# A two-layer hybrid encoder: TensorE kept in the recorded order, memory handed out by planned end of use, convolution taps and key copies spread out

## The chip, the cores and the metric

The kernel runs on one core of one Trainium2 chip. The metric is the device time of one execution in microseconds; three executions of the kernel before gave 1992.22, 1995.13 and 1999.15 us, with the median 1995.13.

## What is computed

A trunk of two layers over 256 positions of width 2048, all float32, with a final RMS norm. Each layer, cut to what matters (the rotary and norm details are left out):

```python
h = rms_norm(x, norm_g)
proj = h @ w_in                       # 2048 x (13*512 + 256 + 4*2048)
ya = a_bg * depthwise_conv(a_cg * a_x, conv_a_w) * silu(a_z)      # A: conv of 3
yb = gqa_attention(rope(q), rope(k), v) * silu(b_z)               # B: 8 heads on 2
yc = rwkv7_bidir(h, c_r, c_k, c_v, ...) * silu(c_z)               # C: a scan per direction
u = depthwise_conv(d_val * sigmoid(d_gate), dw_w) + dw_b          # D: conv of 31 taps
yd = silu(layer_norm(u)) * silu(d_z)
g = sigmoid(gates + b_gate)                                       # 4 x 2048 columns
merged = sum over the branches of g[k] * (y[k] @ w_branch[k])
x = x + merged @ w_out
```

## The kernel before

Activations lie transposed, channels on the partitions and the 256 positions along the free axis. Weights stream in once: 612 pieces of 128 x 1024 (306 per layer), called weight halves here, since two make a tile of 128 output channels. SyncE loads each (`raw`), ScalarE rounds it to a `hi` part, VectorE takes the rest as `lo` (`fetch`), and TensorE multiplies `hi` with both parts of the activations (512 columns) and `lo` with the first part (256 columns), eight of each per half (`tile_b`, `wide`; accumulators `mg`). A merge of a branch takes two such gate tiles and one piece of branch weights (`tile_branch`, accumulator `mb`, 24 matmuls of 256 columns). This is the main stream, in the order of `STREAM`: low-rank inputs, the scan's inputs, k and v, the inputs of B and A, those of D, merges of A and B, gates of D, merge of D, gates of C, merge of C, output projection.

Beside it run side jobs, Python generators: `rwkv` with `inverses` and `chunks`, `branch_a`, `branch_b`, `conv_d`, `branch_d`, `normalise`. Their matmuls write small accumulators, `sd`. After each main matmul `pump` lets those side jobs record a step whose time has come. That time is a plan: `Engine` counts a duration for every operation recorded, keeps a clock for VectorE and ScalarE (`clk`), and sets `due`, the time at which a step's results should be there; a job that yields 0 goes on `SLACK` after it, one that yields a number goes on so much later. Inside `rush` an operation counts as started `BUSY` after the present and is recorded with high priority. `drain` lets planned time pass until a job is done.

The recorded order isn't yet the order of the engines. The framework that builds the program simulates it once and orders each engine's instructions by that simulation and by priority; a main matmul may so be placed ahead of a side matmul recorded before it. `manual_schedule(engines=...)` leaves the named engines in the recorded order; before, only `first_x` does that, and not for TensorE.

The scan is done in chunks of 64 positions, two head pairs at a time. In `rwkv`, per chunk, a matmul makes the next state, ScalarE copies it into a block-diagonal tile (`bdS`), TensorE transposes that (`sd<-consts,bdS`), ScalarE copies the result, and so on: a chain that alternates between TensorE and the other two engines, 48 transpositions in the run. `chunks` prepares the operands of the next pair of chunks; it ends with eight copies of transposed keys and values by ScalarE (`bdE<-sd`). `conv_d` does 31 taps on 128 x 256 for each of four channel groups on VectorE (`arena<-arena,par`).

Short-lived tiles come from one large tile, `arena`, that class `Arena` hands out in units of 32 words. `get` looks for a free gap; before, it prefers a gap that holds nothing freed within the last six calls (`RECENT`), then the tightest.

All operations are recorded through one helper, so nearly all rows of the profile name line 204.

Of the kernel before, what the change touches and what calls it, by code (L numbers as in the profile page):

```python
# [102 lines left out]
class Arena:  # L103


    U = 32
    RECENT = 6

    def __init__(self, ap, words):
        self.ap, self.n = ap, words // self.U  # L110
        self.when = np.zeros(self.n, np.int64)
        self.used = np.zeros(self.n, bool)
        self.live = {}
        self.tick = 0
        self.peak = 0

    def get(self, words, keep=False, take=True):

        m = -(-words // self.U)
        self.tick += 1  # L120
        best = None
        i = 0
        while i < self.n:
            if self.used[i]:
                i += 1
                continue
            e = i
            while e < self.n and not self.used[e]:
                e += 1
            if e - i >= m:  # L130

                j = i if keep else e - m
                key = i if keep else (int(self.when[j:e].max()) > self.tick - self.RECENT, e - i - m, -i)
                if best is None or key < best[0]:
                    best = (key, j)
            i = e
        if best is None:
            if not take:
                return False
            raise MemoryError(f"arena: {words} words asked, {(~self.used).sum() * self.U} free, live "  # L140
                              + str(sorted((v[1] * self.U, v[2]) for v in self.live.values())))
        j = best[1]
        if not take:
            return True
        self.used[j:j + m] = True
        self.peak = max(self.peak, int(self.used.sum()) * self.U * 4)
        return j, m
# [1 line left out]
    def free(self):  # L149
        return int((~self.used).sum()) * self.U  # L150

    def put(self, j, m):
        self.tick += 1
        self.used[j:j + m] = False
        self.when[j:j + m] = self.tick


class Side:
# [6 lines left out]
class Engine:  # L165
# [5 lines left out]
    def __getattr__(self, op):  # L171
        f = getattr(self.real, op)

        def call(out, *args, **kw):
            k = self.k
            if op == "preload_act_table_set":
                k.clk["scalar"] = max(k.clk["scalar"], k.now) + 1.3
                return f(out)  # L178
            if op == "dma_start":
                k.landed = max(k.landed, max(k.due, k.now) + k.DMA)  # L180
            elif self.name == "tensor":
                rhs = kw.get("rhs", args[1])
                n = int(np.prod(out.shape[1:]))
                if op == "transpose":
                    k.now += 0.11
                elif rhs.dtype == F32:
                    k.now += max(0.22, n * 4 / 2400 + 0.003)
                else:
                    k.now += max(0.12, n * 0.4445e-3)
                k.due = max(k.due, k.now + 0.2)  # L190
            else:
                n = max(int(np.prod(x.shape[1:])) for x in (out,) + args if hasattr(x, "shape"))
                cost = 0.06 + n / 960 + (0.07 if op == "scalar_tensor_tensor" else 0) if self.name == "vector" else 0.1 + n / 1200 + (0.09 if hasattr(kw.get("scale"), "shape") or hasattr(kw.get("bias"), "shape") else 0)
                cost *= k.INFL
                if self.name in k.clk:
                    start = max(k.clk[self.name], k.now)
                    k.clk[self.name] = start + cost
                    if k.rushing:
                        start = k.next[self.name] = max(k.next[self.name], k.now + k.BUSY)
                        k.next[self.name] += cost  # L200
                    k.due = max(k.due, start) + cost + 0.1
                else:
                    k.due = max(k.due, k.now) + cost
            return f(out, *args, **kw)  # L204

        return call
# [8 lines left out]
class Kern:  # L215
# [1 line left out]
    FAR = 1  # L217
    INFL = 1.05
    RAW = 8
    BUSY = 0.7  # L220
    SLACK = 0.4
    LEAD = 1.7
    TWAIT = 24.0
    XSTEP = 1.0
# [2 lines left out]
    LEAD_A = 2.0  # L227
    LEAD_B = 1.8
    LEAD_D = 1.0
    DMA = 2.5  # L230
    SLABS = 9
    ARENA = (32 + 474 + 32 + 8 - 8 + 16 - 64 + 128 + 16 + 6 - 88 - 16 - 8 - 16 - 32 * FAR - 32 * PARTS - 16) * 32
# [22 lines left out]
    def a(self, shape, keep=False):  # L255
        words = int(np.prod(shape[1:]))
        if self.cur is None:

            t = self.now
            while not self.arena.get(words, keep, False) and self.now < t + 50:  # L260
                self.now += 0.2
                self.pump()
        j, m = self.arena.get(words, keep)
        if self.cur:
            self.cur.purse.net += m * Arena.U
        ap = self.arena.ap[:, j * Arena.U:j * Arena.U + words]
        if len(shape) > 2:
            names = "abcd"[:len(shape) - 1]
            ap = ap.rearrange(f"p ({' '.join(names)}) -> p {' '.join(names)}",
                              **{k: v for k, v in zip(names, shape[1:])})  # L270
        self.arena.live[id(ap)] = (ap, m, str(shape), j)
        return ap
# [9 lines left out]
    def f(self, *aps):  # L282
        for ap in aps:
            _, m, _, j = self.arena.live.pop(id(ap))
            self.arena.put(j, m)
            if self.cur:
                self.cur.purse.net -= m * Arena.U

# [188 lines left out]
    def whole(self, out, ps):  # L477

        nc = self.nc
        nc.scalar.activation(out, ps[:, 1], AF.Copy)  # L480
        nc.vector.tensor_tensor(out, ps[:, 0], out, ALU.add)
        return out


# [244 lines left out]
    def conv_d(self, acc, i, u):  # L729
# [3 lines left out]
        nc.vector.tensor_scalar(a, u[:, 0:S], w(0), self.dwb2[:, i:i + 1], ALU.mult, ALU.add)  # L733
        for j in range(1, 31):
            nc.vector.scalar_tensor_tensor(a, u[:, j:j + S], w(j), a, ALU.mult, ALU.add)
            if j % 3 == 0:
                yield 0.9
        self.f(u)

    def branch_d(self, acc, convs, dz):  # L740
# [357 lines left out]
    def chunks(self, n, out, bd, al, vv, kb, gs, rd):  # L1098
# [30 lines left out]

        nc.tensor.matmul(ps4[:, 2], vv[:, p, ts], self.cen, start=True, stop=True)  # L1130
        nc.tensor.transpose(ps4[:, 3], al[:, p, ts], self.ident)
        for j, src in enumerate((hi, lo)):
            nc.scalar.activation(ex[hi, j, :, CH:], ps4[src, 0:2, CH:], AF.Copy)
            nc.scalar.activation(ex[lo, j, :, CH:], ps4[src, 0:2, 0:CH], AF.Copy)

        for c, src in enumerate((lo, hi)):
            nc.scalar.activation(ex[hi, 2:4, c, CH:], ps4[src, 2:4, CH:], AF.Copy)
            nc.scalar.activation(ex[lo, 2:4, c, 0:CH], ps4[src, 2:4, 0:CH], AF.Copy)
        out.append((ex, mk, w))
        yield 0  # L1140

# [108 lines left out]
    def merge(self, l, br, g, acc, mT, gens):  # L1250
# [10 lines left out]
        psb = self.tile_branch(self.ys[br])  # L1261
        if first:
            acc[g] = self.a([P, 2, S], True)
            nc.vector.scalar_tensor_tensor(acc[g], z, 1.0, psb, ALU.add, ALU.mult)
        else:
            nc.vector.scalar_tensor_tensor(z, z, 1.0, psb, ALU.add, ALU.mult)
            nc.vector.tensor_tensor(acc[g], acc[g], z, ALU.add)
        self.f(z)
        if last:
# [67 lines left out]
    def run(self):  # L1337
# [2 lines left out]
        self.tiles = 0  # L1340
        self.consts()
        self.first_x()
        for l in range(DEPTH):
            self.layer(l)


@with_exitstack
# [122 lines left out]
```

## Time and profile before

| | us |
|---|---|
| median of three executions | 1995.13 |
| the profiled execution | 1995.8 |
| its span, first to last instruction | 1993.9 |
| TensorE matmul busy | 1934.8 |
| TensorE weight load busy | 1716.7 |
| VectorE busy | 1439.8 |
| ScalarE busy | 1268.9 |
| GpSimd busy | 71.6 |

The span is what the rows measure; the execution's own time has 1.9 us around it. Busy time of an engine counts every moment in which one of its instructions is drawn; the end of a matmul is modelled, so two neighbours overlap in the drawing. PE is TensorE, PEld its weight load, DVE VectorE, ACT ScalarE, POOL GpSimd, SP SyncE.

### The profile page before, as it was taken

What the parts mean: (1) busy time and instruction counts of PE and PEld (TensorE: products, weight loads), DVE (VectorE), ACT (ScalarE), POOL (GpSimd) and SP (SyncE); (2) the same over time, 40 slices, a digit from 0 to 9 for tenths busy, and PEclk for the clock granted to TensorE, in tenths of its full rate; (3) what the DMA queues carried; (4) which work ended last, traced back from release to release, by engine and by line L of the source; (5) the groups of instructions that cost most, each with busy time, mean ns of one, the idle gap of its engine ahead of it and who ended that gap; (6) DMA issues with size and microseconds to landing.
All of it is one profiled execution on the core that took longest, in us unless ns stands there. A gap on an engine that the chain in (4) does not pass through costs nothing.

```text
span 1993.9 us, 32440 instructions
## 1 busy us (share of the span) xinstructions
PE 1934.8 (97%) x12194; PEld 1716.7 (86%) x12194; DVE 1439.8 (72%) x2495; ACT 1268.9 (64%) x2293; POOL 71.6 (4%) x117
## 2 busy tenths in 40 slices
PE   8999999899999999999999999998999999999997
PEld 6888788799988898998888887888999989989986
DVE  7867858967787566666677778589787866566655
ACT  6776666567657766554567766766774577565454
POOL 1001010000101000000000010000001100000000
PEclk9999999899999999999999999999999999999998
DMA  7554443344655345566655554533555544456653
GB/s 247 186 181 165 159 156 117 117 165 166 197 181 180 137 150 179 202 206 205 214 186 185 181 169 143 154 114 138 177 171 187 195 143 159 155 184 207 203 190 136
DMA packets 97693, 343.19 MB, mean 172 GB/s; under 512 B 11808, under 2 KB 12192, under 8 KB 97536
## 3 DMA queue, kind: packets, MB, share of 16 engines
q1 hardware_dynamic: 93312, 331.48, 49.1%
q0 software_dynamic: 3648, 8.59, 1.7%
q8 instruction: 96, 1.57, 0.3%
q10 hardware_dynamic: 576, 1.05, 0.1%
q14 instruction: 61, 0.50, 0.1%
HBM read 332.48 MB, written 8.39 MB: 171 GB/s over the span
## 4 chain that ended last, share of the span: by engine, by line
PE 93%; ACT 3%; DVE 2%; DMA 1%; issue 1%; DVEq 0%; SPq 0%; POOL 0%; ACTq 0%; POOLq 0%
PE mg L204 74%; PE sd L204 9%; PE mb L204 9%; DVE arena L204 1%; DVE lo L204 1%; ACT arena L204 1%; ACT bdE L204 1%; DMA raw<-w 1%; ACT hi L204 1%; DMA scratch<-arena 0%; DMA arena<-xT 0%; ACT bdS L204 0%; ACT L178 0%; ACT bdT L204 0%; ACT bdR L204 0%
## 5 line engine op out<-in xcount | busy, mean ns | idle before, releaser
L204 PE MATMUL mg<-slab,hi 128*128 128x512 f32 x4368 | 1113.7, 396 | 17.1 <-DVE slab L204 9.5
L204 DVE TENSOR_TENSOR lo<-raw,hi 128x1024 fp32r<-128x1024 f32 x612 | 746.6, 1221 | 344.1 <-PE mg L204 247.2
L204 PEld LDWEIGHTS mg<-slab,hi 128*128 128x128 f32 x4368 | 789.6, 190 | 160.9 <-DVE slab L204 10.7
L204 ACT ACTIVATE hi<-raw 128x1024 fp32r<-128x1024 f32 x612 | 646.4, 1057 | 440.4 <-PE mg L204 294.7
L204 PE MATMUL mg<-slab,lo 128*128 128x256 f32 x4368 | 618.4, 285 | 1.7 <-DVE lo L204 1.5
L204 PEld LDWEIGHTS mg<-slab,lo 128*128 128x128 f32 x4368 | 585.9, 191 | 37.5 <-DVE lo L204 3.0
L204 DVE TENSOR_TENSOR arena<-arena 128x512 f32<-128x512 f32 (+16 forms) x389 | 166.1, 432 | 35.2 <-ACT arena L204 24.2
L204 DVE SCALAR_TENSOR_TENSOR arena<-arena,par 128x256 f32<-128x256 f32 x346 | 152.2, 479 | 7.8 <-ACT arena L204 6.7
L204 PE MATMUL mb<-slab,hi 128*128 128x256 f32 (+1 forms) x1040 | 156.8, 288 | 1.0 <-DVE slab L204 0.6
L204 PEld LDWEIGHTS mb<-slab,hi 128*128 128x128 f32 x1040 | 141.1, 192 | 5.7 <-DVE slab L204 0.8
L204 DVE TENSOR_TENSOR arena<-mg,arena 128x256 f32<-128x256 f32 x305 | 126.8, 418 | 18.0 <-ACT arena L204 15.3
L204 ACT ACTIVATE arena<-mg 128x256 f32<-128x256 f32 x241 | 89.7, 377 | 67.4 <-PE mg L204 52.3
L204 ACT ACTIVATE arena<-arena 128x256 f32<-128x256 f32 (+4 forms) x195 | 93.5, 497 | 29.5 <-DVE arena L204 26.1
L204 ACT ACTIVATE arena<-arena,b_gate 128x256 f32<-128x256 f32 x128 | 64.0, 503 | 54.9 <-DVE arena L204 54.4
L204 PE MATMUL mb<-slab,lo 128*128 128x256 f32 x528 | 87.2, 286 | 0.0
L178 ACT ACT_TABLE_LOAD x62 | 79.5, 1283 | 8.3 <-PE sd L204 5.0
L204 PEld LDWEIGHTS mb<-slab,lo 128*128 128x128 f32 x528 | 75.1, 192 | 1.6
L204 ACT ACTIVATE bdE<-sd 64x128 f32<-64x128 f32 x256 | 69.7, 272 | 7.5 <-PE sd L204 4.2
L204 DVE SCALAR_TENSOR_TENSOR slab<-arena,slab 128x512 fp32r<-128x512 f32 (+1 forms) x64 | 35.4, 555 | 34.8 <-ACT slab L204 34.7
L204 ACT ACTIVATE arena<-sd 128x64 f32<-128x64 f32 (+4 forms) x122 | 40.0, 332 | 17.3 <-PE sd L204 15.5
L204 DVE SCALAR_TENSOR_TENSOR arena<-arena 128x256 f32<-128x256 f32 (+1 forms) x80 | 37.1, 473 | 17.6 <-ACT arena L204 16.9
L204 PE MATMUL sd<-arena,bdE 128*128 128x128 f32 (+1 forms) x224 | 45.4, 285 | 3.9 <-ACT arena L204 3.3
(96 smaller groups left out, 1062.2 us busy)
## 6 DMA issues: line engine op xcount, KB each, us to landing
raw<-w SPq DMA_DIRECT2D x612, 512.0 KB, 3.3
arena<-xT SPq DMA_DIRECT2D x4, 512.0 KB, 8.3
scratch<-slab POOLq DMA_DIRECT2D x16, 128.0 KB, 2.7
scratch<-arena POOLq DMA_DIRECT2D x8, 256.0 KB, 4.2
arena<-xT SPq DMA_DIRECT2D x8, 256.0 KB, 3.8
x<-arena SPq DMA_DIRECT2D x8, 256.0 KB, 4.8
arena<-x SPq DMA_DIRECT2D x8, 256.0 KB, 3.6
arena<-lorab POOLq DMA_DIRECT2D x16, 96.0 KB, 2.9
```

What stands on the lines that cost most here:

```text
L178: return f(out)
L204: return f(out, *args, **kw)
```

## The change

Six things are edited.

- TensorE keeps the recorded order through both layers (`manual_schedule` around the layers).
- `Arena` remembers for each unit the planned time at which its last use ends: the latest of now, `due` and the two engine clocks, plus `OVER` = 1.5. `get` prefers places whose time has passed, then the tightest gap; long-lived tiles, too, now prefer such places.
- The plan: `BUSY` goes from 0.7 to 1.2, and an operation of ScalarE on fewer than 128 partitions counts 0.07 more.
- `conv_d` yields after each tap (`TAP` = 1.0), where it yielded 0.9 after every third.
- `chunks` orders its eight copies of transposed keys by destination half and yields 0.6 between the two groups of four.
- The copies out of the main accumulators (`whole`) and the multiplication that frees the branch accumulator (`merge`) are recorded with high priority.

```diff
-                key = i if keep else (int(self.when[j:e].max()) > self.tick - self.RECENT, e - i - m, -i)
+                late = self.when[j:j + m].max() > now
+                key = (late, j) if keep else (late, e - i - m, -i)
...
-    def put(self, j, m):
-        self.tick += 1
+    def put(self, j, m, when):
         self.used[j:j + m] = False
-        self.when[j:j + m] = self.tick
+        self.when[j:j + m] = when
...
-    BUSY = 0.7
+    BUSY = 1.2
     SLACK = 0.4
+    OVER = 1.5
...
+    TAP = 1.0
...
-        j, m = self.arena.get(words, keep)
+        j, m = self.arena.get(words, keep, now=self.now)
...
-            self.arena.put(j, m)
+            self.arena.put(j, m, max(self.now, self.due, *self.clk.values()) + self.OVER)
...
-        nc.scalar.activation(out, ps[:, 1], AF.Copy)
-        nc.vector.tensor_tensor(out, ps[:, 0], out, ALU.add)
+        with self.tc.high_priority():
+            nc.scalar.activation(out, ps[:, 1], AF.Copy)
+            nc.vector.tensor_tensor(out, ps[:, 0], out, ALU.add)
...
             nc.vector.scalar_tensor_tensor(a, u[:, j:j + S], w(j), a, ALU.mult, ALU.add)
-            if j % 3 == 0:
-                yield 0.9
+            yield self.TAP
...
-        for j, src in enumerate((hi, lo)):
-            nc.scalar.activation(ex[hi, j, :, CH:], ps4[src, 0:2, CH:], AF.Copy)
-            nc.scalar.activation(ex[lo, j, :, CH:], ps4[src, 0:2, 0:CH], AF.Copy)
-
-        for c, src in enumerate((lo, hi)):
-            nc.scalar.activation(ex[hi, 2:4, c, CH:], ps4[src, 2:4, CH:], AF.Copy)
-            nc.scalar.activation(ex[lo, 2:4, c, 0:CH], ps4[src, 2:4, 0:CH], AF.Copy)
+        for h, (dst, cols) in enumerate(((lo, slice(0, CH)), (hi, slice(CH, P)))):
+            for j, src in enumerate((hi, lo)):
+                nc.scalar.activation(ex[dst, j, :, CH:], ps4[src, 0:2, cols], AF.Copy)
+
+            for c, src in enumerate((lo, hi)):
+                nc.scalar.activation(ex[dst, 2:4, c, cols], ps4[src, 2:4, cols], AF.Copy)
+            if h == 0:
+                yield 0.6
...
-        for l in range(DEPTH):
-            self.layer(l)
+
+        with self.tc.manual_schedule(engines={mybir.EngineType.PE}):
+            for l in range(DEPTH):
+                self.layer(l)
```

How the order of the instructions moves, at one place of the first layer's forward scan. There `sd` tiles numbered 36xx to 38xx belong to the side jobs, `mg` and `mb` to the main stream, `bdS` is the state's block-diagonal tile, `bdE` and `bdM` are operands of the chunks, and the slabs named with `sd` hold keys and values. TensorE before:

```order
L204 MATMUL sd_3699<-bdR_91,slab_679 128x128 x2
L204 MATMUL sd_3709<-consts,slab_679 128x128 x2
L204 MATMUL sd_3709<-consts,slab_681 128x128 x2
L204 MATMUL sd_3724<-arena,bdE_85 128x128
L204 MATMUL sd_3724<-arena 128x128
L204 MATMUL sd_3751<-consts,bdS_97 128x128
L204 MATMUL sd_3777<-arena,bdE_85 128x64
L204 MATMUL sd_3790<-bdE_83,bdT_77 128x128 x2
L204 MATMUL mb_3898<-slab_1304,hi_3807 128x256 x8
```

and after:

```order
L202 MATMUL sd_3757<-consts,slab_681 128x128 x2
L202 MATMUL sd_3757<-consts,slab_683 128x128 x2
L202 MATMUL mg_3746<-slab_208,hi_3669 128x512
L202 MATMUL sd_3767<-arena,bdE_85 128x128
L202 MATMUL sd_3767<-arena 128x128
L202 MATMUL mg_3746<-slab_208,hi_3669 128x512 x3
L202 MATMUL mg_3746<-slab_207,lo_3670 128x256 x4
L202 MATMUL mg_3746<-slab_208,lo_3670 128x256 x4
L202 MATMUL mg_3746<-slab_209,hi_3696 128x512 x4
L202 MATMUL sd_3799<-consts,bdS_97 128x128
L202 MATMUL mg_3746<-slab_210,hi_3696 128x512 x4
```

Before, the state's matmuls (two into `sd_3724`) are followed at once by the transposition of their result (`sd<-consts,bdS_97`) and more side matmuls; after, one main matmul stands ahead of them (into `sd_3767`) and fifteen between them and the transposition.

VectorE at the same place, where `lo` rows are the weight splits and `arena<-arena,par` on 128 x 256 are taps; before:

```order
L204 SCALAR_TENSOR_TENSOR arena<-arena,par_71 128x256 x6
L204 TENSOR_TENSOR lo_3845<-raw_3805,hi_3844 128x1024
L204 SCALAR_TENSOR_TENSOR arena<-arena,par_71 128x256 x6
L204 TENSOR_TENSOR lo_3902<-raw_3842,hi_3901 128x1024
L204 SCALAR_TENSOR_TENSOR arena<-arena,par_71 128x256 x6
L204 TENSOR_TENSOR lo_3947<-raw_3899,hi_3946 128x1024
L204 TENSOR_TENSOR arena<-sd_3478,rd 128x64
L204 TENSOR_TENSOR arena<-sd_3478,consts 128x64
L204 SCALAR_TENSOR_TENSOR arena<-arena,par_71 128x256 x12
L204 TENSOR_TENSOR arena<-sd_3695,bdE_85 128x192
```

and after:

```order
L202 SCALAR_TENSOR_TENSOR arena<-arena,par_71 128x256 x3
L202 TENSOR_TENSOR lo_3629<-raw_3594,hi_3628 128x1024
L202 SCALAR_TENSOR_TENSOR arena<-arena,par_71 128x256 x2
L202 SCALAR_TENSOR_TENSOR arena<-arena,mb_3625 128x512
L202 SCALAR_TENSOR_TENSOR arena<-arena,par_71 128x256
L202 TENSOR_TENSOR lo_3670<-raw_3626,hi_3669 128x1024
L202 SCALAR_TENSOR_TENSOR arena<-arena,par_71 128x256 x4
L202 TENSOR_TENSOR arena<-sd_3725,rd 128x2x64
L202 TENSOR_TENSOR arena<-sd_3725,consts 128x64
L202 SCALAR_TENSOR_TENSOR arena<-arena,par_71 128x256
L202 TENSOR_TENSOR arena<-sd_3730,bdE_85 128x192
```

The runs of taps between two weight splits, or ahead of a result that the scan needs, are 6, 6, 6 and 12 long before, and at most 4 long after.

ScalarE, the copies of the keys (`bdE<-sd`) and of the state (`bdS<-sd`); before:

```order
L204 ACTIVATE arena<-sd_3638 128x192
L204 ACTIVATE bdM_89<-slab_680 64x2x64 x2
L204 ACTIVATE bdE_83<-sd_3709 64x2x64 x8
L204 ACTIVATE bdS_97<-sd_3724 64x64 x2
L204 ACTIVATE arena<-sd_3724 128x64
L204 ACTIVATE arena<-mg_3732 128x256
L204 ACTIVATE arena<-mg_3804 128x256
```

and after:

```order
L202 ACTIVATE bdM_89<-slab_682 64x2x64 x2
L202 ACTIVATE arena<-mg_3666 128x256
L202 ACTIVATE bdE_83<-sd_3757 64x2x64 x8
L202 ACTIVATE bdS_97<-sd_3767 64x64 x2
L202 ACTIVATE arena<-sd_3767 128x64
L202 ACTIVATE hi_3791<-raw_3747 128x1024
L202 ACTIVATE arena<-arena,b_gate_190 128x256
```

Here the eight copies still stand in one run ahead of the state's two. In the whole program there are 24 runs of eight before and 22 after.

## Rows read from the trace of the kernel before

**Rows 1.** Part 1 of the page: busy us (share of the span) and instructions.
```profile
PE 1934.8 (97%) x12194; PEld 1716.7 (86%) x12194; DVE 1439.8 (72%) x2495; ACT 1268.9 (64%) x2293; POOL 71.6 (4%) x117
```

**Rows 2.** The core's span and its mean granted TensorE clock.
```profile
core 0: 1993.9 us, clock 0.989
```

**Rows 3.** Part 5 of the page: groups of instructions by line.
```profile
L204 PE MATMUL mg<-slab,hi 128*128 128x512 f32 x4368 | 1113.7, 396 | 17.1 <-DVE slab L204 9.5
...
L204 DVE TENSOR_TENSOR lo<-raw,hi 128x1024 fp32r<-128x1024 f32 x612 | 746.6, 1221 | 344.1 <-PE mg L204 247.2
...
L204 ACT ACTIVATE hi<-raw 128x1024 fp32r<-128x1024 f32 x612 | 646.4, 1057 | 440.4 <-PE mg L204 294.7
...
L204 PE MATMUL mb<-slab,lo 128*128 128x256 f32 x528 | 87.2, 286 | 0.0
```

**Rows 4.** The chain that ended last: shares by line, then pieces (start, us, what).
```profile
by line: PE mg L204 74.2%; PE sd L204 9.2%; PE mb L204 9.1%; DVE arena L204 1.1%; issue 0.8%; DVE lo L204 0.8%; ACT arena L204 0.7%; ACT bdE L204 0.7%; DMA raw<-w 0.6%; ACT hi L204 0.6%; DMA scratch<-arena 0.4%; DMA arena<-xT 0.3%; ACT bdS 
...
9.46 20.28 PE mg L204 x96
...
487.71 2.80 PE mg L204 x16
...
490.52 2.87 PE mb L204 x24
```

**Rows 5.** Busy us by stretch: first column length, then engines, clock, DMA.
```profile
350.00:400.00 50.00, 42.19 (x252) 37.51 (x251) 49.52 (x112) 28.91 (x64) 0.00 (x0) 0.90 0.32 112
...
800.00:850.00 50.00, 50.00 (x313) 45.13 (x312) 29.56 (x37) 26.13 (x36) 0.00 (x0) 1.00 0.62 212
...
1300.00:1350.00 50.00, 47.73 (x291) 42.45 (x290) 46.17 (x101) 34.44 (x80) 0.00 (x0) 0.95 0.34 117
```

**Rows 6.** The same view of short stretches around changes of the clock.
```profile
245.00:252.00 7.00, 6.73 (x39) 5.89 (x40) 6.68 (x20) 4.96 (x11) 0.82 (x1) 1.00 0.39 143
...
301.00:308.00 7.00, 6.32 (x28) 6.04 (x29) 3.99 (x13) 4.17 (x14) 0.00 (x0) 0.51 0.24 77
...
1352.00:1356.00 4.00, 3.80 (x11) 3.02 (x12) 4.00 (x12) 1.07 (x3) 0.00 (x0) 0.57 0.40 131
...
1981.00:1994.00 13.00, 0.04 (x1) 0.00 (x0) 5.83 (x6) 2.17 (x3) 3.43 (x2) 0.61 0.43 162
```

**Rows 7.** TensorE's timeline: start, us, what, [idle before <-releaser].
```profile
245.27 0.96 PE L204 MATMUL mg<-slab,hi 128*128 128x512 f32 x3 [1.45 <-DVE arena L204]
...
301.26 0.47 PE L204 MATMUL sd<-consts,bdS 128*128 128x128 f32 x1 [2.28 <-ACT bdS L204]
...
392.88 0.33 PE L204 MATMUL sd<-consts,bdS 128*128 128x128 f32 x1 [2.36 <-ACT bdS L204]
...
1215.73 0.46 PE L204 MATMUL sd<-part,rounded 128*128 128x256 f32 x1 [3.00 <-ACT part L204]
...
1352.20 1.05 PE L204 MATMUL mg<-slab,hi 128*128 128x512 f32 x2 [3.53 <-DVE arena L204]
...
1980.34 0.70 PE L204 MATMUL sd<-arena,consts 128*128 128x256 f32 x2 [0.99 <-ACT arena L204]
```

**Rows 8.** Who waited for whom: us in total, times, longest.
```profile
PE sd L204 <- ACT bdS L204: 10.7, 8, 2.4
...
PE sd L204 <- ACT part L204: 3.7, 2, 3.0
...
DVE arena L204 <- DMA scratch<-arena: 2.8, 1, 2.8
```

**Rows 9.** Timelines of VectorE (first row) and ScalarE between 376 and 398 us.
```profile
382.97 4.83 DVE L204 SCALAR_TENSOR_TENSOR arena<-arena,par 128x256 f32<-128x256 f32 x12
...
390.10 2.26 ACT L204 ACTIVATE bdE<-sd 64x128 f32<-64x128 f32 x8 [1.75 <-PE sd L204]
...
392.37 0.45 ACT L204 ACTIVATE bdS<-sd 64x64 f32<-64x64 f32 x2
```

More of the change, by code (lines that the diff above doesn't have):

```diff
@@ L106, with get @@
     U = 32
-    RECENT = 6
     def __init__(self, ap, words):
         self.ap, self.n = ap, words // self.U
-        self.when = np.zeros(self.n, np.int64)
+        self.when = np.zeros(self.n)
         self.used = np.zeros(self.n, bool)
         self.live = {}
-        self.tick = 0
         self.peak = 0
-    def get(self, words, keep=False, take=True):
+    def get(self, words, keep=False, take=True, now=0.0):
         m = -(-words // self.U)
-        self.tick += 1
         best = None
@@ L150, in free @@
         return int((~self.used).sum()) * self.U
-    def put(self, j, m):
-        self.tick += 1
+    def put(self, j, m, when):
         self.used[j:j + m] = False
-        self.when[j:j + m] = self.tick
+        self.when[j:j + m] = when
 class Side:
@@ L192, in call @@
                 n = max(int(np.prod(x.shape[1:])) for x in (out,) + args if hasattr(x, "shape"))
-                cost = 0.06 + n / 960 + (0.07 if op == "scalar_tensor_tensor" else 0) if self.name == "vector" else 0.1 + n / 1200 + (0.09 if hasattr(kw.get("scale"), "shape") or hasattr(kw.get("bias"), "shape") else 0)
+                cost = 0.06 + n / 960 + (0.07 if op == "scalar_tensor_tensor" else 0) if self.name == "vector" else 0.1 + n / 1200 + (0.09 if hasattr(kw.get("scale"), "shape") or hasattr(kw.get("bias"), "shape") else 0) + (0.07 if out.shape[0] < P else 0)
                 cost *= k.INFL
@@ L1263, in merge @@
             acc[g] = self.a([P, 2, S], True)
-            nc.vector.scalar_tensor_tensor(acc[g], z, 1.0, psb, ALU.add, ALU.mult)
-        else:
-            nc.vector.scalar_tensor_tensor(z, z, 1.0, psb, ALU.add, ALU.mult)
+        with self.tc.high_priority():
+            nc.vector.scalar_tensor_tensor(acc[g] if first else z, z, 1.0, psb, ALU.add, ALU.mult)
+        if not first:
             nc.vector.tensor_tensor(acc[g], acc[g], z, ALU.add)
```

## The prediction

> **What bounds the kernel now.** First the busy shares. TensorE's matmul row is busy 1934.8 of 1993.9 us [rows 1], so everything that the change can win is time in which TensorE waits, or runs at half its clock. I sized that in three ways.
>
> Waits that show as idle: 1993.9 - 1934.8 = 59.1 us. The first matmul starts at 9.46 us [rows 4] and the last one ends at 1980.34 + 0.70 = 1981.0 [rows 7], so 9.5 us of start and 12.9 us of tail are no waits of this kind and stay. 36.7 us are left.
>
> Clock: the mean granted clock is 0.989 [rows 2], so 0.011 x 1993.9 = 21.9 us were not granted. 13 x 0.39 = 5.1 us of it lie in the tail after the last matmul [rows 6]. The other 17 us come from six stretches of 3.5 to 7 us at half clock, 1.2 GHz in place of 2.4; the first and the last of them are in [rows 6], the four between, from 383, 393, 1216 and 1298 us, read alike. Each begins as a wait of TensorE of 2.28 to 3.53 us ends (four of the six in [rows 7]). After the wait of 1.45 us at 245 us the clock stayed full [rows 6, 7].
>
> A floor from undisturbed pieces: 16 matmuls of half a weight tile (8 of 512 columns, 8 of 256) take 2.80 us, the 24 of a branch tile 2.87 us [rows 4]. There are (4368 + 16)/8 = 548 of the first and (528 - 16)/8 = 64 of the second [rows 3]; the 16 belong to the fourth tile of the run, which uses the branch tiles' buffer: 1534.4 + 183.7 us. Side matmuls (tile name sd) are 9.2% of the chain, 183.4 us. With 9.5 and 12.9 us that makes 1923.9 us. The kernel took 1993.9, so **70 us are lost**: 36.7 idle, 17 to the clock, and 16 in waits too short to show, because a 512-column matmul is drawn 396 ns long [rows 3] while its neighbours start about 230 ns apart (eight of them in 2.80 - 8 x 0.12 us).
>
> The Trainium skill (Perfetto Trace Analysis, Identifying the Most-Contended Engine) says that matmul busy time is a poor measure of headroom and that weight-load busy time should be used. By that page: 1716.7 us in all [rows 1] at the 45.13/50 of the smooth stretch [rows 5] is 1902 us, an estimate; the trace agrees that the 3% of idle time understates the headroom.
>
> Where the 70 us sit: VectorE is busy 49.52 of 50 us from 350 us and 46.17 from 1300 us, and there TensorE falls to 42.19 and 47.73 at clocks of 0.90 and 0.95; in the smooth stretch it is 50.00 at 1.00 [rows 5].
>
> **Part 1, TensorE's order and the later due times (BUSY).** Before, a transposition of the recurrent state stands directly behind the matmuls that make the state, with ScalarE's copy between them: such waits are 10.7 us in total [rows 8]. At 392.88 us TensorE idles 2.36 us [rows 7] because ScalarE does eight key copies first (2.26 us) and then the state copy (0.45 us) [rows 9]. In the new order one 512-column matmul stands ahead of the state's matmuls, and seven of 512 and eight of 256 columns behind them: together 8 + 8, 2.80 us [rows 4], against the 2.26 + 0.45 = 2.71 us that ScalarE needs. So that wait goes, with nothing late next, by a margin of 0.1 us plus the two side matmuls. The chain gets longer in matmuls between steps, yet its last transposition of the first layer moves up from weight half 222 to 216 in the order (the branch that needs it begins at 234), so no merge becomes late. What the fixed order costs: no matmul is chosen around a late one, so at every late copy the whole main stream stands behind it, and the weight splits on VectorE and ScalarE, which wait for buffers, stand behind that.
>
> **Part 2, taps one by one.** Before, taps of the long convolution stand in runs of up to 12 on VectorE; twelve took 4.83 us [rows 9], in the stretch where VectorE is at 49.52 of 50. The order has 12 runs of five or more before and 2 after, none over five: 5/12 x 4.83 = 2.0 us at most. VectorE's total is unchanged, and its weight split alone is 1221 ns for each 2.80 us [rows 3, 4]. In the two stretches VectorE is still at its limit, so I let 7 us of waits stay there (bounds 2 and 20: nothing but one run of five per stretch, or all of today's loss).
>
> **Part 3, key copies in two groups.** The order says that this hardly happens: runs of eight copies go from 24 to 22. Priced at 0; bounds -2 and +2 us, one run of eight [rows 9] saved or added on TensorE's path.
>
> **Part 4, memory and priorities.** Memory given out later can end waits of an engine for a transfer that still reads it. The nearest row is VectorE's wait for a scratch transfer, 2.8 us, once [rows 8]; it delays TensorE only where VectorE is the bound. The copies out of the accumulators move ahead in their queues. I take 0, with bounds of -3 and +3.
>
> **Sum.** What stays of the 70: waits on the two-step split of a side operand (3.7 us in 2 waits on its first half [rows 8]; the new order has little between there), 5 us, bounds 0 and 10; taps, 7; half of the 16 us of short waits, 8; clock 0, bounds 0 and 7 (two falls), since no wait left should reach 2.28 us. 20 us in all: 1923.9 + 20 = 1943.9 us of span, and the 1995.8 - 1993.9 = 1.9 us around it give **1946 us**. The profiled execution (1995.8) stands 0.03% over the median, so no correction is made. All lower bounds together give 1930, the upper bounds with all 16 us of short waits 1923.9 + 10 + 20 + 16 + 7 + 5 + 1.9 = 1984.
>
> **Rivals.** VectorE stays the bound: in the two stretches all of today's loss comes back, since the taps are only spread, not fewer. That is idle 7.8 + 2.3 us, clock 5.0 + 2.5 us [rows 5], and the 3.53 us wait at 1352 us with its fall, 1.7 us: 22.8 in place of 7, so 1962 us, and about 1966 with a few short waits more. For it: 49.52 of 50. Against it: the taps that were bunched there are what filled those 50 us.
>
> Slower: the head of the line. If ScalarE's copies come later than the main matmuls put between allow (the key copies still stand ahead of them in runs of eight), each of the 48 transpositions waits as eight do today, 10.7/8 = 1.34 us [rows 8]: 64 us, so 1923.9 + 20 + 64 + 1.9 = 2010 us, and more with the clock. It decides from a mean wait of (70 - 20)/48 = 1.0 us. For it: a margin of 0.1 us is thin, and a weight split of 1057 ns [rows 3] can come in between. Against it: these copies have priority, and many of the 48 have no key copies ahead. The Trainium skill (TensorE: Matmul & The Clock Gate, Part 2) says that matmuls stay in program order and only weight loads are pulled ahead; by that the price of the rival stands in full, and the rows of idle time agree as far as they go.
>
> No change: VectorE and ScalarE keep orders of their own, so what the spacing saves at the side steps can come back as waits for weight splits. That needs 50 us to be given back: 1990 to 2000 us. Against it: at 2.80 us for each half tile, splits of 1221 and 1057 ns [rows 3, 4] leave both engines half free outside the two stretches.
>
> **How the numbers follow.** Forecast 0.68, VectorE the bound 0.16, no change 0.05, slower 0.07, and 0.04 for a time under 1930, if all waits vanish and the side matmuls lose the half-clock time that their 183 us contain. Range 1930 to 1972: the lower bounds, and the VectorE rival with 6 us to spare; the forecast's upper bounds beyond that, and the last two cases, are left out. About 0.3% (6 us) is what a measurement of this kernel can tell from no change. Faster by more: 0.68 + 0.16 + 0.04 = 0.88; within: 0.05; slower: 0.07.
>
> **What would show it.** Idle of TensorE between first and last matmul near 15 us instead of 36.7; no wait on the state copy over 1 us; a mean clock of 0.996 or more, with only the tail at half; 350 to 400 us with TensorE above 47. I am wrong if six or more half-clock stretches remain, if waits on side copies sum to over 20 us, or if the weight splits on VectorE become what TensorE waits for.

## The result, and the profile after

The changed kernel took **2015.21 us**, the median of four executions (2011.95 to 2017.58), beside 1995.95 (1992.22 to 1999.15) of the kernel before on the same chip: 1.0096 times as long, interval 1.0072 to 1.0120. The forecast was 1946 with a range of 1930 to 1972. It was wrong in sign as well as in size. Times are medians of all executions; one of the four of the kernel with the split delay (below) took 2117.32 us at a mean clock of 0.847, and without it that median is 1982.47 us in place of 1982.59.

The profiled execution took 2011.95 us, 3.3 below the median. Part 1 of its page, the core's span and clock, and the list of what TensorE (PE) waited for (us in total, times, longest); line 202 is the helper's line, 204 in the kernel before:

```profile
PE 1934.0 (96%) x12194; PEld 1707.4 (85%) x12194; DVE 1447.7 (72%) x2495; ACT 1261.3 (63%) x2293; POOL 71.3 (4%) x117
```
```profile
core 0: 2009.7 us, clock 0.990
```
```profile
PE sd L202 <- DVE arena L202: 18.8, 3, 9.7
PE mg L202 <- DVE slab L202: 12.7, 5, 9.6
PE sd L202 <- DVE part L202: 10.2, 17, 1.3
PE sd L202 <- ACT part L202: 9.7, 10, 1.7
PE sd L202 <- ACT bdT L202: 4.3, 4, 1.3
PE sd L202 <- ACT arena L202: 4.1, 4, 2.2
PE sd L202 <- ACT bdE L202: 2.3, 1, 2.3
PE sd L202 <- ACT bdS L202: 1.3, 4, 0.4
```

TensorE's work is the same (1934.0 beside 1934.8 us busy [rows 1]); the waits are others. The last row is what the change removed: 10.7 us on the state's copies became 1.3, the longest 0.4 [rows 8]. The wait of 9.6 us in the second row is the start of the kernel. Without it the eight rows sum to 53.8 us, which is all idle time between the first and the last matmul (36.7 before). 18.8 us stand behind VectorE (DVE) in three waits, 19.9 us in 27 waits for the two-step split of a side operand (`part`), where [rows 8] had 3.7 in 2 on its first half.

Busy time by stretch (column order as in [rows 5]):

```profile
350.00:400.00 50.00, 47.69 (x319) 43.23 (x319) 48.84 (x104) 33.63 (x82) 0.66 (x1) 1.00 0.44 139
550.00:600.00 50.00, 40.48 (x258) 36.40 (x256) 41.98 (x88) 21.36 (x35) 3.29 (x6) 0.96 0.54 173
800.00:850.00 50.00, 50.00 (x311) 45.10 (x310) 31.34 (x40) 26.46 (x38) 0.00 (x0) 1.00 0.62 207
1300.00:1350.00 50.00, 48.97 (x309) 43.39 (x308) 49.19 (x107) 36.98 (x87) 0.00 (x0) 1.00 0.46 148
1550.00:1600.00 50.00, 41.51 (x244) 36.88 (x242) 40.95 (x81) 21.65 (x38) 5.08 (x8) 0.90 0.51 164
```

The two stretches that the prediction worked on are mended: 42.19 to 47.69 and 47.73 to 48.97 us of TensorE, at a clock of 1.00 [rows 5]. The loss turned up where nothing was lost before, at 600 us and at the same place of the second layer. The kernel before in those two stretches:

```profile
550.00:600.00 50.00, 50.00 (x314) 45.07 (x313) 44.66 (x92) 26.67 (x42) 0.00 (x0) 1.00 0.52 180
1550.00:1600.00 50.00, 50.00 (x309) 45.02 (x307) 40.59 (x74) 26.69 (x44) 5.18 (x8) 1.00 0.61 197
```

The first of them after the change, in the timeline (start, us, what, and in brackets the idle time before and its end):

```profile
590.34 3.76 DVE L202 TENSOR_TENSOR arena<-arena 64x175 f32<-64x175 f32 x13
594.14 1.03 DVE L202 COPY arena<-arena 64x1024 f32<-64x1024 f32 x1
594.66 0.61 POOL L202 DMA_DIRECT2D scratch<-arena  x1 [53.46 <-DVE arena L202]
...
599.02 1.15 DVE L202 TENSOR_TENSOR arena<-arena 128x512 f32<-128x512 f32 x2 [3.86 <-DMA scratch<-arena]
600.22 0.50 PEld L202 LDWEIGHTS sd<-arena,consts 128*128 128x128 f32 x2 [10.16 <-DVE arena L202]
600.22 1.22 PE L202 MATMUL sd<-arena,consts 128*128 128x256 f32 x2 [9.74 <-DVE arena L202]
```

The matmuls at 600.22 are the sums of branch D's layer norm. They need the two adds at 599.02, and these stand on VectorE behind the last 13 steps of the scan's inversion, its final copy, and a wait of 3.86 us for memory that the transfer to `scratch` still reads. The second layer has the same at 1591.62 us, 8.49 us of idle time. The kernel before had the same queue on VectorE:

```profile
600.99 1.13 DVE L204 COPY arena<-arena 64x1024 f32<-64x1024 f32 x1
...
604.61 1.12 PE L204 MATMUL mb<-slab,hi 128*128 128x256 f32 x8
604.95 0.69 DVE L204 TENSOR_TENSOR arena<-arena 128x512 f32<-128x512 f32 x1 [2.83 <-DMA scratch<-arena]
```

There TensorE goes on with main matmuls (604.61) while VectorE waits, because the framework had put the sums behind them. The recorded order does not. The Trainium skill (TensorE: Matmul & The Clock Gate, Part 2) has matmuls stay in program order; the idle 9.74 us agree.

A split wait reads like this. ScalarE (ACT) has two table loads of 1.28 us, with one other operation between them, ahead of the first half of the split, so TensorE stands:

```profile
137.83 1.28 ACT L176 ACT_TABLE_LOAD   x1
...
139.62 1.28 ACT L176 ACT_TABLE_LOAD   x1
...
140.91 0.63 ACT L202 ACTIVATE part<-arena 128x512 fp32r<-128x512 f32 x1
...
141.59 0.50 PE L202 MATMUL sd<-part,rounded 128*128 128x512 f32 x1 [1.66 <-ACT part L202]
```

Sorted as the prediction sorted it, where the fourth row is the span less the other three:

| us | before | forecast | after |
|---|---|---|---|
| start and tail | 22.3 | 22.4 | 21.9 |
| idle between | 36.7 | 12 | 53.8 |
| lost at half clock | 17.1 | 0 | 15.4 |
| matmuls and short waits | 1917.8 | 1909.5 | 1918.6 |
| span | 1993.9 | 1943.9 | 2009.7 |

### The profile page after: what moved, and what is told of

Same layout as the page of the kernel before. It is cut to its first block, busy times and chain, and to the rows that moved or that the text cites. A ratio compares the mean times of both kernels' runs of the same rounds, so it can differ in the third digit from the quotient of the medians.

```text
span 2009.7 us, 32327 instructions
## 1 busy us (share of the span) xinstructions
PE 1934.0 (96%) x12194; PEld 1707.4 (85%) x12194; DVE 1447.7 (72%) x2495; ACT 1261.3 (63%) x2293; POOL 71.3 (4%) x117
## 4 chain that ended last, share of the span: by engine, by line
PE 89%; DVE 6%; ACT 2%; DMA 1%; issue 1%; POOL 0%; DVEq 0%; SPq 0%; POOLq 0%; ACTq 0%
PE mg L202 71%; PE mb L202 9%; PE sd L202 9%; DVE arena L202 3%; DVE lo L202 2%; ACT arena L202 1%; ACT hi L202 1%; DVE slab L202 1%; DMA arena<-scratch 1%; DVE part L202 0%; DMA arena<-xT 0%; ACT L176 0%; DMA scratch<-arena 0%; ACT bdE L202 0%; ACT bdT L202 0%
## 5 line engine op out<-in xcount | busy, mean ns | idle before, releaser
L202 PE MATMUL mg<-slab,hi 128*128 128x512 f32 x4368 | 1148.8, 399 | 12.7 <-DVE slab L202 12.7
L202 PEld LDWEIGHTS mg<-slab,lo 128*128 128x128 f32 x4368 | 604.2, 191 | 46.1 <-issue 4.2
L202 PE MATMUL mg<-slab,lo 128*128 128x256 f32 x4368 | 634.1, 286 | 0.0
L202 DVE TENSOR_TENSOR arena<-arena 128x512 f32<-128x512 f32 (+15 forms) x389 | 165.8, 431 | 17.7 <-DMA scratch<-arena 6.4
L202 PE MATMUL mb<-slab,hi 128*128 128x256 f32 (+1 forms) x1040 | 152.0, 286 | 0.0
L202 PEld LDWEIGHTS mb<-slab,hi 128*128 128x128 f32 x1040 | 136.1, 192 | 0.6
L202 ACT ACTIVATE arena<-arena 128x256 f32<-128x256 f32 (+4 forms) x195 | 94.0, 497 | 50.7 <-DVE arena L202 49.9
L202 DVE SCALAR_TENSOR_TENSOR arena<-arena,mb 128x512 f32<-128x512 f32 x64 | 43.8, 685 | 47.2 <-PE mb L202 45.8
L202 ACT ACTIVATE bdE<-sd 64x128 f32<-64x128 f32 x256 | 62.9, 269 | 8.4 <-PE sd L202 5.6
L202 PE MATMUL sd<-part,rounded 128*128 128x512 f32 (+1 forms) x88 | 29.0, 378 | 20.0 <-DVE part L202 10.2
```

## The experiments

Theory F: in a fixed order every side result that comes later than the plan says stops the whole main stream. Theory M: the memory rule and the plan make results late, whatever TensorE's order. All times below are medians beside the kernel before in the same session (1994.7 to 1995.6 us).

### The order alone, and the rest alone

The rest alone is the changed kernel without the fixed order; the order alone is the kernel before with that edit only.

```diff
-        with self.tc.manual_schedule(engines={mybir.EngineType.PE}):
-            for l in range(DEPTH):
-                self.layer(l)
+        for l in range(DEPTH):
+            self.layer(l)
```

> The changed kernel with TensorE's order left to the framework again; the plan, the taps, the memory and the priorities stay as changed. Theory F (the fixed order is what costs: a late side result now stops the main stream): faster than before, 1970 to 1990 us, TensorE's idle between first and last matmul at 20 to 35 us in place of 53, and no wait over 5 us at the layer norm of branch D near 600 and 1590 us. Theory M (the new memory rule and the new plan make VectorE's results late whatever TensorE's order is): 2005 to 2020 us, as slow as the changed kernel.

> The kernel before with one edit, TensorE kept in the recorded order; BUSY 0.7, taps in threes, old memory rule. Theory F: slower than the changed kernel, 2015 to 2040 us, since the plan leaves 0.5 us less for each rushed result and the taps stand in threes. Theory M: about as before, 1990 to 2000 us.

The rest alone: 1984.94 us, 0.9949 (0.9934 to 0.9964). The order alone: 2034.96 us, 1.0192 (1.0175 to 1.0209). So the fixed order costs 39.4 us by itself and 30.3 us on top of the rest, and the rest gains 10.6 or 19.8. F holds. With the order alone VectorE shows why the taps matter there: fourteen of them in a row while a matmul of the scan waits for the VectorE operation behind them, here and at 1395.57 us.

```profile
383.27 5.62 DVE L204 SCALAR_TENSOR_TENSOR arena<-arena,par 128x256 f32<-128x256 f32 x14
...
389.28 0.80 PE L204 MATMUL sd<-arena,bdE 128*128 128x128 f32 x2 [5.81 <-DVE arena L204]
```

The changed kernel has neither wait.

### The two places of the loss

The layer-norm sums later by plan (in `branch_d`, ahead of the adds):

```diff
-        yield 0
+        yield 14.0
         sq = self.a([P, NT, S])
```

> The changed kernel with branch D's layer norm recorded 14 us of planned time later, so that its sums on TensorE stand at weight half 180 and 486 in place of 175 and 481, behind the place where VectorE ends the triangular inversion (178 and 484). Theory F: the two waits of 9.7 and 8.5 us and the two stretches of half clock behind them (about 5 us each) go: 1985 to 1992 us. If the wait only moves along: 2005 to 2015 us.

1996.74 us, 1.0007 (0.9997 to 1.0016): 18.5 us of the 19.7 are gone. In the order the sums moved from weight half 175 to 180, and from 481 to 486, and TensorE waits 0.39 us there:

```profile
604.84 0.70 PE L202 MATMUL sd<-arena,consts 128*128 128x256 f32 x2 [0.39 <-DVE arena L202]
```

Steps behind a two-step split later by plan (end of `parts`):

```diff
         self.nc.vector.tensor_tensor(view(lo), x, view(hi).bitcast(F32), ALU.subtract)
+        self.due += 1.5
         return hi, lo
```

> The changed kernel with 1.5 us more of planned time for the two-step split of a side operand (tile name part). Theory F with the split as the second cost: the waits of TensorE on part fall from 20 us in 27 to under 6 us, and the time by 12 to 16 us, 1998 to 2004 us, unless the layer norm's place moves too. If ScalarE's and VectorE's queues just come later by the same: no change, 2012 to 2018 us.

1982.59 us, 0.9932 (0.9915 to 0.9948), 32.6 us less than the changed kernel and more than I expected, because this edit moved the sums to 180 and 486 as well, and the last copy of the inversion from 176 and 482 to 186 and 492: the sums' adds now run ahead of it, and TensorE does not wait for them. What TensorE waited for:

```profile
PE mg L202 <- DVE slab L202: 12.4, 5, 9.3
PE sd L202 <- ACT arena L202: 12.1, 9, 2.3
PE sd L202 <- ACT bdT L202: 5.0, 4, 1.8
PE sd L202 <- DVE part L202: 3.2, 6, 0.7
PE mg L202 <- DVE arena L202: 1.7, 2, 0.8
```

The split's waits fell from 19.9 to 3.2 us, and the first-half row is gone; waits on ScalarE's other copies took back 8 us. Both edits together tell the two apart.

> The changed kernel with both delays in its plan: the layer-norm sums of branch D 14 us later, and every step behind a two-step split 1.5 us later. Theory A (the two places are separate costs, 18.5 us and 32.6 us by the two runs alone): 2015 - 51 = 1964 us, 1958 to 1970. Theory B (the second delay has already moved the layer-norm sums, from weight half 175 to 180 and from 481 to 486, so the first adds nothing): 1983 us, 1977 to 1988. I hold B the likelier, since the profile with the second delay alone has no wait of TensorE for the layer norm left.

1983.61 us, 0.9939 (0.9921 to 0.9957). Theory B: the second edit holds the first. So the sums cost 18.5 us and the split waits 1996.7 - 1983.6 = 13.1 us, together 31.6.

The place of the sums was then brought back under another plan: the kernel with the split delay, with

```diff
-    BUSY = 1.2
+    BUSY = 0.7
...
```

and without ScalarE's surcharge of 0.07.

> The changed kernel with the steps behind a two-step split 1.5 us later (1982.6 us) and, in addition, the old planned start of a rush (0.7 us). In the order of this kernel the layer-norm sums stand at weight half 175 and 481 again, with the last copy of the inversion at 176 and 482, as in the changed kernel. Theory D (the place decides: TensorE in fixed order waits for sums that stand on VectorE behind the end of the inversion): the two waits of 8 to 10 us come back, 1982.6 + 18 = 2001 us, 1995 to 2006. Theory B (the planned start is what was worth 10.7 us alone, by clock and idle time): 1968 to 1978 us.

2003.88 us, 1.0039 (1.0024 to 1.0054), as Theory D has it. The queue is back:

```profile
588.86 1.15 DVE L202 TENSOR_TENSOR arena<-arena 128x512 f32<-128x512 f32 x2 [4.70 <-DMA scratch<-arena]
...
590.07 1.22 PE L202 MATMUL sd<-arena,consts 128*128 128x256 f32 x2 [7.90 <-DVE arena L202]
```

### Single parts done alone

The kernel before with one edit each: taps one by one, and the new memory rule.

```diff
-            if j % 3 == 0:
-                yield 0.9
+            yield self.TAP
```

> The kernel before with one edit alone: the long convolution yields after each tap. Theory T (the prediction's: of the loss in the two stretches where VectorE is full, 20 us and more, 13 to 15 us go): 1995.5 - 14 = 1981 us, 1978 to 1986, with TensorE above 45 us of 50 from 350 to 400 us. Theory R (VectorE has the same work in those stretches, so the loss moves with it): 1990 to 2000 us.

1997.73 us, 1.0017 (1.0008 to 1.0027): Theory R. Of the waits in [rows 7] the one at 393 us is gone and the one at 1352 us shrank to 1.2, and the first of the two stretches is mended as the prediction had it (42.19 to 48.81 us, clock 0.90 to 1.00), the second hardly:

```profile
350.00:400.00 50.00, 48.81 (x326) 44.46 (x326) 48.17 (x102) 37.02 (x87) 0.00 (x0) 1.00 0.42 137
1300.00:1350.00 50.00, 47.82 (x295) 42.88 (x296) 45.01 (x98) 36.51 (x87) 0.00 (x0) 0.97 0.36 119
```

But a merge waited instead:

```profile
459.51 1.83 PE L204 MATMUL mb<-slab,hi 128*128 128x256 f32 x7 [12.97 <-DVE arena L204]
```

```diff
-                key = i if keep else (int(self.when[j:e].max()) > self.tick - self.RECENT, e - i - m, -i)
+                late = self.when[j:j + m].max() > now
+                key = (late, j) if keep else (late, e - i - m, -i)
...
```

> The kernel before with one edit alone: memory is handed out by the planned end of its last use. Theory T (the prediction's: worth nothing within 3 us): 1992 to 1999 us. Theory M (waits of VectorE and ScalarE for memory still in use are what fills them in the two stretches): most of the 10.6 us that all the edits but the fixed order give comes from here, 1983 to 1989 us.

2013.71 us, 1.0096 (1.0077 to 1.0114). Neither theory: the rule alone loses 19 us in the free order. Its idle time is 49.9 us and its half-clock loss 23.9, 20 us more than before in all, spread over single waits of 2 to 5 us from 230 us on.

### Single parts undone

The changed kernel with taps in threes, the old memory rule, the old plan (`BUSY` and surcharge), or ordinary priority of the copies out of the accumulators:

```diff
-            yield self.TAP
+            if j % 3 == 0:
+                yield 0.9
```

> The changed kernel with one part undone: the long convolution yields 0.9 after every third tap again. Theory T (under the fixed order the spread taps are what ended the two waits of 5.97 us, at 389 and 1396 us, that the kernel with only the fixed order shows, each with 6.8 us at half clock): these come back, 2 x (6 + 3.4) = 19 us, so 2015 + 19 = 2034 us, 2024 to 2040. Theory D (what counts is where the layer-norm sums fall beside the last operations of the inversion: without the single taps they come at weight half 177 and 483, with the copy that ends the inversion behind them, at 185 and 491): the two waits of 9 us at the layer norm go, and the time is 1996 to 2012 us.

2000.60 us, 1.0030 (1.0020 to 1.0040), faster than with the taps spread: Theory D. No wait at the sums is left. Fourteen taps in a row are back on VectorE, and beside them a wait of TensorE of 3.81 us in the first layer and 3.80 in the second, each with 6.8 us at half clock:

```profile
343.46 5.64 DVE L202 SCALAR_TENSOR_TENSOR arena<-arena,par 128x256 f32<-128x256 f32 x14
343.77 1.04 ACT L202 ACTIVATE hi<-raw 128x1024 fp32r<-128x1024 f32 x1
344.84 1.00 ACT L202 ACTIVATE bdE<-sd 64x128 f32<-64x128 f32 x4
347.15 0.37 ACT L202 ACTIVATE arena<-sd,arena 128x128 f32<-128x128 f32 x1 [1.31 <-DVE arena L202]
347.57 0.80 PE L202 MATMUL sd<-arena 128*128 128x128 f32 x2 [3.81 <-ACT arena L202]
```

Of the 3.81 us ScalarE spends 2.1 on a weight split and four key copies and waits 1.31 for VectorE, so Theory T's mechanism is at most a third of this wait (and the waits that it speaks of are 5.81 us in the trace, not 5.97). Beside the kernel with only the sums delayed (1996.7), which has no such wait at the sums either, this one is 4 us slower; how much of that is the taps is not shown.

```diff
-                late = self.when[j:j + m].max() > now
-                key = (late, j) if keep else (late, e - i - m, -i)
+                key = i if keep else (int(self.when[j:e].max()) > self.tick - self.RECENT, e - i - m, -i)
...
```

> The changed kernel with one part undone: memory is handed out by the old rule (the last six calls, then the tightest gap). Theory T (the prediction's, worth nothing within 3 us): 2012 to 2018 us. Theory M (the new rule costs what it cost alone under the free order, 18.9 us, by placing tiles so that they wait for each other): 1993 to 2000 us.

2015.65 us, 1.0102 (1.0082 to 1.0123). The size is Theory T's, the reason isn't: the sums' adds now stand ahead of the inversion's end on VectorE, so TensorE no longer waits for them, but the inversion's result lands late and TensorE waits for that (1609.41 us likewise).

```profile
616.05 0.31 PE L205 MATMUL sd<-bdX,slab 64*32 64x32 f32 x2 [5.08 <-DMA bdX<-scratch]
```

```diff
-    BUSY = 1.2
+    BUSY = 0.7
...
```

> The changed kernel with one part undone: an operation in a rush counts as started 0.7 us after the present (1.2 in the changed kernel) and a small ScalarE operation costs no 0.07 us more. Theory F (side results come later than planned, so an earlier plan makes it worse): the waits on the state's copies and on the operands of the scan grow, 2022 to 2040 us. Rival (the scan's steps have enough main matmuls between them either way): 2010 to 2020 us.

2004.55 us, 1.0042 (1.0028 to 1.0056). Both theories missed: the inversion's copy moved ahead, to weight half 171 and 477, four before the sums, and their wait went.

```diff
-        with self.tc.high_priority():
-            nc.scalar.activation(out, ps[:, 1], AF.Copy)
-            nc.vector.tensor_tensor(out, ps[:, 0], out, ALU.add)
+        nc.scalar.activation(out, ps[:, 1], AF.Copy)
+        nc.vector.tensor_tensor(out, ps[:, 0], out, ALU.add)
...
```

> The changed kernel with one part undone: the copies out of the main accumulators and the multiplication that frees the branch accumulator have ordinary priority again. Theory T (the prediction's, worth nothing within 3 us): 2012 to 2018 us. Theory P (with TensorE in a fixed order an accumulator that comes free late stops the main stream, so these copies are worth much): 2022 us or more, with waits of TensorE's mg or mb matmuls on VectorE.

2014.34 us, 1.0099 (1.0083 to 1.0115): worth nothing, as predicted.

### The memory rule in two more surroundings

The edit of the undone rule again, now in the kernel with the split delay, and in the one without the fixed order.

> The changed kernel with the steps behind a two-step split 1.5 us later (1982.6 us), and with the old rule for memory. Theory T (memory is worth nothing, and the layer-norm sums, at weight half 180 and 486, have enough ahead of them either way): 1979 to 1986 us, no wait on bdX over 1 us. Theory W (with the old rule the inversion ends later, and the transfers of its result into bdX, which TensorE waited 5.1 us for in each layer with the old rule alone, land late again): 1992 to 2004 us.

1991.57 us, 0.9979 (0.9970 to 0.9988), between the theories: no wait on `bdX`, but waits of 1.9 to 2.5 us on splits, sums and scan operands.

> The changed kernel without the fixed order (1984.9 us) and with the old rule for memory, so that taps, due times, key copies and priorities are left of the change. Theory M (the new rule costs in the free order what it costs alone there, 18.9 us): 1962 to 1970 us, and this is the fastest kernel. Theory T (what an edit is worth depends on where the other edits put the steps; nothing adds): within 6 us of 1985.

2011.88 us, 1.0080 (1.0063 to 1.0097): both theories wrong. The rule that costs 19 us alone (18.9 in the expectations) saves 27 us here. Taking edits out one by one gives no price for an edit in this kernel.

### Everything later

```diff
-    SLACK = 0.4
+    SLACK = 1.2
```

in the kernel with both delays.

> The changed kernel with both delays, and in addition every side step that waits for its inputs is recorded 1.2 us after its planned due time in place of 0.4. Theory F (what is left of the loss is still results that come later than planned: with the split delay alone TensorE waits 12.1 us for ScalarE's copies into arena tiles, 5.0 for bdT and 3.2 for the splits): these 20 us fall below 8, and the time to 1966 to 1974 us. Theory L (the chain of the scan gets longer by 0.8 us at each of its steps, so what waits at the end of it is late): the side waits fall too, but one wait of several us shows at a merge, and the time is 1980 to 2000 us.

2170.37 us, 1.0879 (1.0863 to 1.0895). Theory L in kind, ten times its size: the inversion's copy moved from weight half 186 to 240, so the scan came when the main stream had nothing left to put beside it, and TensorE waited 31 us for `bdX` and then stepped through the scan alone, mostly at half clock (a mean of 0.63 from 792 to 870 us, where no main matmul runs). Its stretch from 750 us, and the waits for those transfers:

```profile
750.00:800.00 50.00, 16.23 (x200) 14.34 (x199) 29.22 (x76) 10.90 (x23) 5.79 (x10) 0.66 0.27 78
```
```profile
PE sd L202 <- DMA bdX<-scratch: 62.9, 4, 31.3
```

### What the runs say together

In four kernels with the recorded order on TensorE the sums stand in it at weight half 175 and 481, and on VectorE their adds come right behind the end of the inversion: the changed one, the order alone, ordinary priorities, and the split delay with the old plan. Each of them waits 7.7 to 9.7 us at the sums in each layer (in the second layer of the order alone, at the second sum, that of the squares). The order alone has the old memory rule, so the new rule is not what makes this wait. In the eight other kernels with a fixed order, where the sums come later, the copy earlier, or the adds ahead of it, no such wait is over 2 us. That mechanism is shown. Why the memory rule changes sign with its surroundings is not: the traces show that the steps fall in another order, and long waits in other places, and no run isolates one of them. The plan, the priorities and the key copies were not run alone in the free order, so their own prices are open.

The fastest kernels are the split delay (1982.6 us), both delays (1983.6) and the rest alone (1984.9), 0.5 to 0.7% under the kernel before and not to be told apart.

## Why the prediction was wrong, point by point

**What held.** The state's copies: 10.7 to 1.3 us, the longest 0.4; with the order alone they are 3.3, so the order did most of it. The taps: the two stretches came to 47.69 and 48.97 us; what idles there, 2.3 and 1.0 us, is less than the 7 that were left for it. The reading of the first stretch was right, since the taps alone mend it in the free order too. The step from there to the total was not: the time that they won came back at a merge and in other waits, and the kernel was no faster. Priorities at 0 held. Memory at 0 came out by luck: undone it makes 0.4 us, because one wait went and another came, and alone it costs 19. The later due times, which part 1 counts with the order, make this kernel slower: with the old plan it takes 10.7 us less. Of the signs that the prediction named, no wait on the state copy over 1 us and more than 47 us from 350 to 400 us came true. The others went against it: idle time is 53.8 us, the clock 0.990, and the waits on side copies, where it called over 20 us a sign of being wrong, are 31.9 us besides the sums'.

**The step that failed: "no merge becomes late" stood for all that could be late.** Part 1 looked at the scan's copies, where the new order has a spare half tile, and said of other late copies only that the main stream would stand behind them. I gave that sentence no price. It is the head-of-line rival, right in mechanism and wrong in its place: I put it at the 48 state transpositions (64 us), where it costs 1.3 us. It was at the sums of branch D (18.2 us of idle time against 0 in the sum) and at the splits. That the rival's 2010 us stands near the measured 2015 is luck.

**Part 4's row was the clue.** "It delays TensorE only where VectorE is the bound" was said of the 2.8 us that VectorE waits for the scratch transfer [rows 8]. That held only while TensorE could be given other work. Followed one step on, to the next matmul that needs VectorE's result, it would have led to 600 us.

**Split waits, 5 us with bounds 0 and 10: 19.9 us.** I sized them by the waits of the kernel before, 3.7 us in 2. But those were few because main matmuls had been put ahead of the late ones: with the same edits and the free order, TensorE waits 3.5 us in 4 for splits. A row of the free order is no price for the fixed one.

**Clock, 0 with bounds 0 and 7: 15.4 us.** I let it go with the waits over 2.28 us. New waits brought new falls: 10.2 us at half clock at each layer's sums, and three stretches of 3.4 us. Those three came after waits of 1.26, 2.18 and 1.26 us, so the six waits of the kernel before were no measure. With only the sums delayed the loss fell to 8.5 us.

**Half of the 16 us of short waits: nothing.** The fourth row of the table is 1917.8 us before and 1918.6 after, and 1908 to 1927 in the other kernels but the one with everything later. None of these orders removed more than 9.3 us of it. So the floor that I subtracted (1923.9 us with start and tail) was too low as a target; that its side matmuls, priced by their share of the chain, are the reason is not shown.

**The sum.** Idle 53.8 instead of 12, clock 15.4 instead of 0, matmuls 9.1 more than 1909.5, start and tail 0.5 less: 65.8 us, the distance of the spans 2009.7 and 1943.9. (The lower bounds add up to 1930.8, not 1930, which changes nothing.) Delaying the two places leaves 1983.6 us. In the kernel with the split delay alone, the 37 us between its span (1980.7) and the forecast's 1943.9 are 29.2 us idle instead of 12, 11.9 at half clock, and 8.5 of the floor, less 0.8 of start and tail: the forecast was out of reach even without the two places.

The chances were as wrong as the sum. 0.07 for slower rested on one place being safe, and the order lists 48 transpositions but many more matmuls that wait for a side result.

## What to carry to other kernels

When an engine gets a fixed order, price every instruction in it that needs another engine's result, not only the chain one had in mind; a wait that the free order covers can show in the old trace as idle time of the engine that produces (here 2.83 us of VectorE's), not of the one that consumes. A plan's margin must fit the operation: 1.5 us at the splits gained 13 us, 0.8 us everywhere lost 187 because the longest chain ran out of cover. And where an order is generated, the price of an edit is the price of the places that it moves, so look for the long waits in the new trace and move those, rather than judge edits one by one.

## What I had not expected of the hardware

Falls of the clock do not go by the length of the wait just before. Busy time in four stretches of the changed kernel (clock in the third column from the right):

```profile
64.60:68.00 3.40, 3.36 (x19) 2.94 (x20) 2.58 (x5) 2.71 (x5) 0.24 (x1) 1.00 0.45 165
281.00:285.00 4.00, 2.74 (x72) 2.01 (x71) 0.96 (x1) 3.36 (x6) 0.00 (x0) 1.00 0.42 131
285.20:288.60 3.40, 3.40 (x15) 3.11 (x14) 0.00 (x0) 2.81 (x5) 0.00 (x0) 0.50 0.01 2
...
1585.60:1595.80 10.20, 4.18 (x14) 3.75 (x15) 4.89 (x13) 2.47 (x6) 5.08 (x8) 0.50 0.38 98
```

A wait of 1.73 us ends at 64.64 and the clock stays at 2.4 GHz. At 284.46 one of 1.26 us ends, and 0.7 us later it is at 1.2 GHz; of TensorE's 72 matmuls in the 4 us from 281, 64 were the scan's of 32 columns, and it was busy for 2.74 us. A wait of 2.31 us that ends at 361.84 is followed by no fall: the stretch from 350 to 400 us, shown above, is at 1.00. At the sums of the second layer it falls while TensorE still waits and stays down for 10.2 us, 4.18 of them busy, until 4.2 us past the end of the wait. So in these rows the last wait alone does not tell whether the clock falls; no run isolates what does.

The same 512-column matmuls start 231 ns apart (median) in every kernel with a fixed order and 229 to 230 in the free ones. From one matmul to the next the names of the tiles change 2089 to 2103 times in the fixed ones (1999 in the one with everything later) and 1915 to 1966 times in the free ones. The means differ by some 0.75 ns, which is 3 us over 4368 matmuls. No run looked for the cause.
